# Matmul with rotary embedding on one core: two more block pairs, one queue for all quarter loads, and small warm-up matmuls

## The chip, the cores and the metric

The kernel runs on one core of one Trainium2 chip. The metric is the device time of one execution in microseconds. An execution was also profiled; the profile's span runs from the first to the last instruction, and the rest of the device time lies around it.

The engines go by two names here: PE is TensorE (matmuls; PEld its weight loads), DVE is VectorE, ACT is ScalarE, POOL is GpSimd, SP is SyncE, which issues DMAs and computes nothing.

## The reference

`x` has 16 batches of 512 rows of 768 float32 values, `weight` is 768 x 768, `cos` and `sin` are 512 x 64, and there are 12 heads of 64.

```python
y = np.matmul(x, weight).reshape(batch, seq, n_heads, head_dim)
y1, y2 = y[..., :32], y[..., 32:]
out1 = y1 * cos1 - y2 * sin1
out2 = y2 * cos2 + y1 * sin2
out = np.concatenate([out1, out2], axis=-1).reshape(batch, seq, hidden)
```

`cos1` and `cos2` are the two halves of `cos`, the same for each batch and head; so are `sin1` and `sin2`.

## The kernel before

**Tiles.** The 8192 rows of `x` are 64 tiles of 128 rows, in 16 groups of four (`QB = 4`): tile 4g + s is in group g. A group has the same quarter of the sequence for four batches. A pair is two neighbouring tiles, written (g, h): (6, 0) is tiles 24 and 25, (6, 1) is 26 and 27.

**Two ways to turn a tile.** The contraction needs `x` transposed. An ordinary tile is loaded whole by SyncE into one of `NX` buffers `xs` (`load`), cast to fp16 by ScalarE into `xc` (`cast`), transposed on TensorE with the identity into the PSUM tile `pt`, and copied by ScalarE into `xt` (`turn`, or from tile 6 on `turn_rows`, twelve 64 x 64 transposes on halves of the rows). A *block pair* is loaded in four quarters (`load_quarter`), so placed that a transpose of 32 x 32 blocks on VectorE (`turn_pair`, L303) finishes the work, into one of `NXP` buffers `xp`; it takes no TensorE time and no PSUM. A block pair of SyncE's arrives as float32 in one of `NB` buffers `xb` and is cast by ScalarE into one of two buffers `xd` (`cast_pair`); one of GpSimd's is converted to fp16 by the DMA on its way into one of `NBH` buffers `xh`, and has no cast. `BLOCKS` names the block pairs and who loads them; before, they are (3,1), (5,1), (7,1), (8,0), (8,1), (9,1), (10,0), (10,1), (11,1), (12,1), (13,1) and (15,1) on SyncE, (4,1) and (6,1) on GpSimd.

**Matmuls and products.** From tile 4 on the matmuls (L365, `walk` and `both`) run as two interleaved lines, one on each half of the contraction rows, and fill three PSUM banks per half group, the other three serving the next half; the first and last tiles use L340. When a unit of columns is complete, VectorE multiplies it by cos and sin in one instruction (`rope`, L446), from PSUM into `tq` or the no longer needed `w_raw`. GpSimd adds the two products (L468) into one of four output buffers `ov`; in the last group VectorE and TensorE do some of the sums. ScalarE issues most stores, SyncE the last ones.

**What sets the order.** All is written by hand: `do` appends an instruction to its engine's queue and adds the semaphore waits that its tiles need. The main loop goes over tiles i = 4 to 63 and writes the matmuls of tile i, the block transposes of pairs that begin before tile i + 4 (`B_AHEAD`), turns 3 tiles ahead, casts 5 ahead, and GpSimd's loads 20 ahead. SyncE's loads follow the list `fetch`; `pump` sends on from it as long as a buffer of the kind is written off. Pairs in `EARLY` have their quarters in their tiles' place in that list; other SyncE pairs (`soon`) have theirs spread between the tile loads before.

**The start.** While the first loads are under way, TensorE multiplies zeros (`warm`, L582, the tile `cold`): nine matmuls of 128 x 512, the turn of tile 0, three more, the turn of tile 1. The last six of the twelve also clear the banks that the first matmuls add to. The six weight chunks are cast by VectorE as they land, and the first four tiles' matmuls follow chunk by chunk.

Of the kernel before, what the change touches and what calls it, by code (L numbers as in the profile page):

```python
# [16 lines left out]
class Flow:  # L17
# [24 lines left out]
    def do(self, e, make, reads=(), writes=(), dma=None, tick=True, after=0):  # L42
        need = {}
        for k in reads:
            for s, v in self.wrote.get(k, {}).items():
                need[s] = max(need.get(s, 0), v)
        for k in writes:
            for d in (self.wrote, self.readby):
                for s, v in d.get(k, {}).items():
                    need[s] = max(need.get(s, 0), v)  # L50
        if e == "pe":
            need.pop("pe", None)
            if after:
                need["pe"] = after
        waits = self.settle(e, need)
        for s, v in waits[:-1]:
            self.eng[e].wait_ge(self.sem(s), v)  # L57
        i = make(self.eng[e])
        if waits:
            s, v = waits[-1]  # L60
            i.wait_op(self.sem(s), v, "sem-ge")
        name, step = (dma, 16) if dma else (e, 1)
        self.sem(name)
        self.order[name] = len(self.order) + sum(self.count.values())
        at = self.count[name] + step
        if tick or dma:
            i.then_inc(self.sems[name], step)
            self.count[name] = at
            self.known[name, at] = dict(self.seen[e])
        for k in reads:  # L70
            d = self.readby.setdefault(k, {})
            d[name] = max(d.get(name, 0), at)
        for k in writes:
            self.wrote[k] = {name: at}
            self.readby[k] = {}
        return i
# [32 lines left out]
def kernel(  # L109
# [11 lines left out]
    f = Flow(nc, tc)  # L121
    do = f.do
    P = nc.NUM_PARTITIONS
# [13 lines left out]
    LAST = NG - 1  # L137


    BLOCKS = {}  # L140
    for g in range(5, 14):
        BLOCKS[g, 1] = "pool" if g % 2 == 0 and g >= 4 else "sp"
    BLOCKS[LAST, 1] = "sp"
    BLOCKS[4, 1] = "pool"
    EARLY = ((3, 1), (8, 0), (8, 1), (9, 1), (10, 0), (10, 1), (11, 1), (12, 1), (13, 1))
    for p in EARLY:
        BLOCKS[p] = "sp"

    def sbuf(name, shape, dt):
        return nc.alloc_sbuf_tensor(name, shape, dt).ap()  # L150

    NX, NB, NBH, NC, NCP, NXT, NXP, NOV = 10, 3, 3, 5, 2, 8, 4, 4

    ident = sbuf("ident", [P, P], FP16)
    cold = sbuf("cold", [P, 512], FP16)
# [26 lines left out]
    py = nc.alloc_psum_tensor("py", [P, 6 * 512], FP32).ap()  # L182
# [14 lines left out]
    def where(i):  # L197
        g, s = divmod(i, QB)
        return QB * (g // SB) + s, g % SB

    def pair_of(i):
        return i // QB, (i % QB) // 2

    def is_block(i):
        return pair_of(i) in BLOCKS

# [11 lines left out]
    def load_quarter(gh, q):  # L218
        g, h = gh
        b, r = where(g * QB + 2 * h)  # L220
        e = BLOCKS[gh]
        src = x[b : b + 2].rearrange("b (j a r) (q k) -> r q a (b j) k", r=SB, a=R, q=NQ)
# [282 lines left out]
    def store_half(g, h, c, at):  # L505
# [20 lines left out]
       reads=["ident"], writes=["ident32"])  # L526
# [13 lines left out]
    fetch, quarters = [], []  # L540
    soon = [p for p in sorted(BLOCKS) if BLOCKS[p] == "sp" and p not in EARLY]
    for i in range(QB, NTILE):
# [3 lines left out]
        if not is_block(i):  # L546
            fetch.append(i)
            for _ in range(2 if i == QB * (LAST - 1) else 1):
                if quarters:
                    fetch.append(quarters.pop(0))  # L550
        elif pair_of(i) in EARLY:
            fetch += [(pair_of(i), q) for q in ((0, 2), (1, 3))[i % 2]]
# [23 lines left out]
    WARM = 12  # L576
    warmed = [0]

    def warm(k):
        for _ in range(k):  # L580
            b = warmed[0] % 6
            do("pe", lambda eng: eng.matmul(  # L582
                py[:, ts(b, 512)], cold[:, 0:P], cold, start=True, stop=warmed[0] < WARM - 6),
                reads=["cold"], writes=[f"ps{b}"], tick=False)
            warmed[0] += 1

    def mm0(i, c):
# [10 lines left out]

    U0 = units(0)
    warm(9)  # L600
    castx(0, "act")
    turn(0, "dve")
    castx(1, "act")
    warm(3)
    turn(1, "dve")
    castx(2, "act")
# [13 lines left out]
    for c in CHUNKS[3:5]:  # L620
# [8 lines left out]
        reads=["sin", "csn1", "cos"], writes=["csn"])  # L629
# [74 lines left out]
    for i in range(QB, NTILE):  # L704
        g, s = divmod(i, QB)
# [16 lines left out]
        for n, p in enumerate(pieces(g, s)) if i >= ROWS else ():  # L722
# [3 lines left out]
            for c in CHUNKS:  # L726
                mm_piece(i, p, c, c == CHUNKS[0], c == CHUNKS[-1],
                         tick=c == CHUNKS[-1])
# [60 lines left out]
```

## Time and profile before

| | |
|---|---|
| Time, median of 3 runs | 150.32 us (149.86 to 150.71) |
| The profiled execution's own time | 148.68 us |
| Its span | 146.9 us |
| TensorE, VectorE, GpSimd, ScalarE busy | 140.0, 128.0, 116.7, 76.5 us |
| Granted TensorE clock | 1.00 in all windows |
| Bytes moved | 52.44 MB, mean 357 GB/s |
| DMA issues: whole tiles, quarters, GpSimd's quarters | 36, 48, 8 |

In the page, the groups of instructions give busy time, mean nanoseconds of one, and the idle time of the engine just before them. The chain of waits goes back from the last instruction to what released it. Timelines list start and length of merged runs of instructions; a bracket tells how long the engine had been idle before and what ended that. Windows give each engine's busy time in a stretch, then the granted clock, the share of the DMA engines and GB/s.

### The profile page before, as it was taken

The page shows a single profiled execution, that of the slowest core. Times are in us where ns is not written, and L with a number is a line of the kernel's source. Part 1 is how long each engine was busy: PE and PEld are TensorE (multiplying, and loading weights), DVE is VectorE, ACT ScalarE, POOL GpSimd, SP SyncE. Part 2 cuts the span into 40 slices and gives each one's busy share as a digit, 9 for nine tenths or more (in the row PEclk, how much of TensorE's full clock was granted, in tenths as well). Part 3 has the DMA queues.
Part 4 walks back from the last instruction along what each step waited for, and adds up shares of the span by engine and source line. Part 5 has one row for each costly group of instructions (what it writes and reads, how often), then busy time and mean ns, then how long its engine had stood idle before and what let it go on. Part 6 is the DMA issues. An engine that isn't in the chain of part 4 may idle for free.

```text
span 146.9 us, 4261 instructions
## 1 busy us (share of the span) xinstructions
PE 140.0 (95%) x1846; PEld 112.1 (76%) x1846; DVE 128.0 (87%) x105; ACT 76.5 (52%) x84; POOL 116.7 (79%) x64
## 2 busy tenths in 40 slices
PE   6969999999999999999999999999999999999980
PEld 2445578888888888888888888888888888765860
DVE  0155999878989999899999999999989899999990
ACT  3453798788242933557442942284664649931010
POOL 2000399999996988959788988989899999899980
PEclk9999999999999999999999999999999999999999
DMA  4999999999999999999999999999999999999684
GB/s 118 379 403 404 402 401 270 263 332 327 329 332 330 339 390 389 383 345 375 377 386 384 389 395 387 396 392 393 385 388 398 392 404 401 394 412 360 267 314 158
DMA packets 37826, 52.44 MB, mean 357 GB/s; under 512 B 4656, under 2 KB 31024, under 8 KB 37808
## 3 DMA queue, kind: packets, MB, share of 16 engines
q1 hardware_dynamic: 21200, 30.42, 59.2%
q10 hardware_dynamic: 14432, 20.97, 38.6%
q0 software_dynamic: 2176, 0.79, 4.3%
q8 instruction: 14, 0.23, 0.6%
q14 instruction: 4, 0.03, 0.1%
HBM read 27.79 MB, written 25.17 MB: 361 GB/s over the span
## 4 chain that ended last, share of the span: by engine, by line
PE 83%; DVE 12%; issue 2%; DVEq 0%; SPq 0%
PE py L365 69%; DVE tq L446 8%; PE py L340 5%; PE py L582 4%; PE pt L275 3%; DVE w_raw L446 2%; PE pt L260 2%; DVE ov L415 1%; DVE py L408 0%; DVE xs L408 0%; DVE xt L194 0%; DVE w_sb L194 0%; DVE cold L519 0%; DVEq L57 0%; DVEq L784 0%
## 5 line engine op out<-in xcount | busy, mean ns | idle before, releaser
L468 POOL TENSOR_TENSOR ov<-tq 128x512 f32<-128x512 f32 (+3 forms) x34 | 76.1, 2258 | 22.4 <-DVE tq L446 21.8
L446 DVE TENSOR_TENSOR tq<-py,csn 128x1024 f32<-128x1024 f32 (+2 forms) x51 | 74.2, 1491 | 2.9 <-PE py L365 1.9
L365 PE MATMUL py<-w_sb,xt 64*128 64x512 f16 (+1 forms) x672 | 64.1, 323 | 0.0
L365 PE MATMUL py<-w_sb,xp 64*128 64x256 f16 (+1 forms) x624 | 58.7, 323 | 0.0
L365 PEld LDWEIGHTS py<-w_sb,xt 64*128 64x128 f16 x672 | 47.3, 94 | 8.8 <-DVE tq L446 0.4
L365 PEld LDWEIGHTS py<-w_sb,xp 64*128 64x128 f16 x624 | 44.2, 94 | 7.2
L194 ACT COPY xt<-pt 128x768 f16<-128x768 f16 x34 | 27.1, 801 | 33.2 <-PE pt L275 31.3
L194 ACT CAST xc<-xs 128x768 f16<-128x768 f32 x36 | 32.5, 910 | 18.3 <-PE py L365 10.5
L468 POOL TENSOR_TENSOR ov<-w_raw 128x1536 f32<-128x1536 f32 (+2 forms) x15 | 35.4, 2372 | 3.0 <-DVE w_raw L446 2.9
L446 DVE TENSOR_TENSOR w_raw<-py,csn 128x1024 f32<-128x1024 f32 (+1 forms) x22 | 35.2, 1600 | 2.5 <-PE py L365 2.1
L194 ACT CAST xd<-xb 128x1536 f16<-128x1536 f32 x12 | 19.6, 1632 | 4.0 <-PE py L365 4.0
L340 PE MATMUL py<-w_sb,xt 128*128 128x256 f16 (+1 forms) x102 | 16.8, 317 | 1.1 <-DVE w_sb L194 1.1
L340 PEld LDWEIGHTS py<-w_sb,xt 128*128 128x128 f16 x102 | 9.4, 98 | 6.7 <-DVE w_sb L194 2.0
L275 PEld LDWEIGHTS pt<-ident,xc 64*128 64x128 f16 x360 | 11.6, 95 | 1.2 <-issue 0.2
L275 PE MATMUL pt<-ident,xc 64*128 64x64 f16 x360 | 11.6, 190 | 0.0
L303 DVE STREAM_TRANSPOSE xp<-xd 128x768 f32<-128x768 f32 x12 | 11.6, 966 | 0.0
L582 PE MATMUL py<-cold 128*128 128x512 f16 x12 | 5.5, 630 | 1.4 <-DVE cold L519 1.4
L194 DVE COPY xt<-pt 128x768 f16<-128x768 f16 x2 | 1.1, 558 | 5.8 <-PE pt L260 5.8
L194 DVE CAST w_sb<-w_raw 128x768 f16<-128x768 f32 x6 | 3.3, 557 | 2.7 <-DMA w_raw<-in_weight_dram 2.6
L194 ACT COPY ov<-py 128x256 f32<-128x256 f32 x1 | 0.4, 372 | 10.0 <-PE py L478 10.0
L229 POOL DMA_DIRECT2D xh<-in_x_dram x8 | 4.8, 601 | 0.0
L582 PEld LDWEIGHTS py<-cold 128*128 128x128 f16 x12 | 1.6, 145 | 3.6 <-issue 2.2
(26 smaller groups left out, 24.5 us busy)
## 6 DMA issues: line engine op xcount, KB each, us to landing
out_dram<-ov ACTq DMA_DIRECT2D x53, 384.0 KB, 7.6
xs<-in_x_dram SPq DMA_DIRECT2D x36, 384.0 KB, 11.7
xb<-in_x_dram SPq DMA_DIRECT2D x48, 192.0 KB, 10.5
out_dram<-ov SPq DMA_DIRECT2D x4, 768.0 KB, 6.0
w_raw<-in_weight_dram SPq DMA_DIRECT2D x6, 384.0 KB, 7.0
xh<-in_x_dram POOLq DMA_DIRECT2D x8, 96.0 KB, 15.3
out_dram<-ov SPq DMA_DIRECT2D x1, 384.0 KB, 2.3
out_dram<-ov SPq DMA_DIRECT2D x3, 128.0 KB, 2.1
```

What stands on the lines that cost most here:

```text
L194: eng.copy(out=o, in_=i_) if e == "act" else eng.tensor_copy(out=o, in_=i_)
L229: do(e, lambda eng: eng.dma_start(out=dst[ts(q, R)], in_=src[r, q]), writes=[f"{name}q{q}"], dma=name)
L260: do("pe", lambda eng: eng.transpose(pt[:, t, h, :], src[:, t, h, :], ident), reads=[f"xc{c}", "ident"], writes=[f"pt{k}"], tick=(t, h) == ...
L275: do("pe", lambda eng: eng.transpose(pts[r][:, t, h, :], src[rows, t, h, :], ident[rows, rows]), reads=[f"xc{c}", "ident"], writes=[f"pt{r ...
L303: do("dve", lambda eng: eng.transpose(out=dst, in_=src), reads=rd, writes=[f"xp{z}"])
L340: do("pe", lambda eng: eng.matmul(ps, get(t, h), w_sb[:, t, h, a - s * H : z - s * H], start=start, stop=stop), reads=[key, f"w{t}{h}"], w ...
L365: do("pe", lambda eng: eng.matmul(py[:, a:z], get(t, h)[rows], w_sb[rows, t, h, a - s * H : z - s * H], start=start, stop=not opens and en ...
L415: do("dve", lambda eng: eng.tensor_tensor(out=ov_b[o][:, ds(c0, w)].rearrange("p (h t d) -> p h t d", t=2, d=HD), in0=q.rearrange("p (h t ...
L446: do("dve", lambda eng: eng.tensor_tensor(out=tq.rearrange("p j (h d) -> p j h d", d=D), in0=ps.rearrange("p (h d) -> p h d", d=D) .unsque ...
L468: do(adder, lambda eng: eng.tensor_tensor(out=ov_b[o][:, ds(c0, w)].rearrange("p (h t d) -> p h t d", t=2, d=HD), in0=tq[:, 0].rearrange(" ...
L582: do("pe", lambda eng: eng.matmul(py[:, ts(b, 512)], cold[:, 0:P], cold, start=True, stop=warmed[0] < WARM - 6), reads=["cold"], writes=[f ...
```

## The change

Three parts:

- There are sixteen block pairs instead of fourteen: (6,0) and (12,0) are new, so tiles 24, 25, 48 and 49 are no longer turned on TensorE.
- All are SyncE's. (4,1) and (6,1) move from GpSimd to SyncE and get a cast on ScalarE. All but (15,1) have their quarters in their tiles' place in the list of loads; (5,1) and (7,1) were spread before. The buffers change with it: `xs` 11 instead of 10, `xb` 4 instead of 3, no `xh`. Loads are 32 whole tiles and 64 quarters.
- The first six of the twelve matmuls of zeros become eight each of 64 rows, 64 weight columns and 64 columns.

```diff
-    BLOCKS = {}
-    for g in range(5, 14):
-        BLOCKS[g, 1] = "pool" if g % 2 == 0 and g >= 4 else "sp"
-    BLOCKS[LAST, 1] = "sp"
-    BLOCKS[4, 1] = "pool"
-    EARLY = ((3, 1), (8, 0), (8, 1), (9, 1), (10, 0), (10, 1), (11, 1), (12, 1), (13, 1))
+    BLOCKS = {(LAST, 1): "sp"}
+    EARLY = ((3, 1), (4, 1), (5, 1), (6, 0), (6, 1), (7, 1), (8, 0), (8, 1), (9, 1), (10, 0), (10, 1), (11, 1), (12, 0), (12, 1), (13, 1))
     for p in EARLY:
         BLOCKS[p] = "sp"
...
-    NX, NB, NBH, NC, NCP, NXT, NXP, NOV = 10, 3, 3, 5, 2, 8, 4, 4
+    NX, NB, NBH, NC, NCP, NXT, NXP, NOV = 11, 4, 0, 5, 2, 8, 4, 4
...
     def warm(k):
         for _ in range(k):
             b = warmed[0] % 6
-            do("pe", lambda eng: eng.matmul(
-                py[:, ts(b, 512)], cold[:, 0:P], cold, start=True, stop=warmed[0] < WARM - 6),
-                reads=["cold"], writes=[f"ps{b}"], tick=False)
+            n = 64 if warmed[0] < WARM - 6 else 512
+            for c in range(0, 512, n):
+                do("pe", lambda eng: eng.matmul(
+                    py[0:min(P, n), ds(b * 512 + c, n)], cold[:, 0:min(P, n)], cold[:, ds(c, n)],
+                    start=True, stop=warmed[0] < WARM - 6),
+                    reads=["cold"], writes=[f"ps{b}"], tick=False)
             warmed[0] += 1
```

## The prediction

> **What bounds the kernel now.** I read the page first, then the chain of waits, the timelines of TensorE, VectorE and ScalarE, and a table of windows. The page:
>
> ```profile
> PE 140.0 (95%) x1846; PEld 112.1 (76%) x1846; DVE 128.0 (87%) x105; ACT 76.5 (52%) x84; POOL 116.7 (79%) x64
> PE 83%; DVE 12%; issue 2%; DVEq 0%; SPq 0%
> ```
>
> Busy PE could still hide pauses, so I went to the chain in order of time (start, length, what):
>
> ```profile
> 1.41 4.02 PE py L582 x9
> 5.43 0.64 PE pt L260 x6
> 6.07 1.25 PE py L582 x3
> 7.32 0.35 PE pt L260 x6
> ...
> 66.18 13.65 PE py L365 x126
> 79.83 0.17 PE pt L275 x10
> ...
> 104.11 1.92 PE py L365 x19
> 106.03 0.20 PE pt L275 x11
> 106.23 5.85 PE py L365 x54
> 112.08 0.17 PE pt L275 x10
> ```
>
> From 8.8 to 124.5 us TensorE runs without a break. Where no tile is turned on it, 126 matmuls (seven tiles of 18) take 13.65 us, 1.95 each. Four tiles of which two are turned take 112.26 - 104.11 = 8.15 us instead of 7.80: a turn costs 0.175 us of TensorE. VectorE, the next one, keeps close behind:
>
> ```profile
> 100.51 0.97 DVE L303 STREAM_TRANSPOSE xp<-xd 128x768 f32<-128x768 f32 x1
> 101.40 5.58 DVE L446 TENSOR_TENSOR tq<-py,csn 128x2048 f32<-128x2048 f32 x3
> 107.45 1.23 DVE L446 TENSOR_TENSOR w_raw<-py,csn 128x1024 f32<-128x1024 f32 x1 [0.46 <-PE py L365]
> ...
> 115.60 2.36 DVE L446 TENSOR_TENSOR tq<-py,csn 128x1024 f32<-128x1024 f32 x2 [0.53 <-PE py L365]
> ```
>
> A block transpose holds it 0.89 us (100.51 to 101.40). The brackets are its pauses for TensorE; from 115.60 to the end at 143.3 it has none over 0.15 us. So the end is set by when VectorE reaches that product, and then by TensorE and VectorE in turn.
>
> **The turns that go.** Tiles 24, 25, 48 and 49 become block pairs (6,0) and (12,0). Their 48 small transposes leave TensorE: 4 x 0.175 = 0.70 us, half near 56 to 58 us, half at 104 to 106. All of it lies on the path.
>
> **VectorE.** Two transposes more, 2 x 0.89 = +1.78 us. The two pairs that GpSimd loaded, (4,1) and (6,1), now read xd; theirs fall from 1.17 (60.39 to 61.56) to 0.89, -0.56. (6,0)'s stands behind group 5's first product (55.30): 0.89 goes into the pauses at 59.25 (0.54) and 67.40 (0.27), the 0.28 saved on (6,1) and the overlap; by 100 us VectorE is some 0.3 ahead of before, as TensorE is 0.35. (12,0)'s stands behind group 11's first product: then 107.45 becomes 107.45 - 0.3 + 0.89 - 0.46 - 0.08 = 107.50 (0.08 is what consecutive instructions overlap when nothing waits), with no pause left, and 115.60 becomes 107.50 + 8.15 - 0.53 - 0.08 = 115.04. TensorE's data would be there at 115.60 - 0.70 = 114.90, so VectorE decides: -0.56 us. TensorE waits for VectorE only when a bank is still being read. In group 9, which has two pairs at once behind it, the product of the last two banks ends at 96.01 and the next matmul into them starts at 96.26: 0.25 us to spare. By the same count group 11's, after the change, ends at 111.71 and TensorE wants them at 112.56 - 0.70 = 111.86: 0.15. Bounds of this term: -0.70 (VectorE hidden) to 0 (each transpose given back); I take -0.56, as groups 7 and 9 have the same order of work and show no pause of TensorE.
>
> **ScalarE, GpSimd, SyncE.** ScalarE loses four casts (0.910) and four copies (0.801), -6.84, and gains four pair casts (1.632), +6.53. The new wait: (6,1)'s and (12,1)'s casts need the xd buffer of two pairs before, that is VectorE's transpose; copies, casts and stores on ScalarE queue behind. The like casts at 70.68 and 86.68 waited 2.0 us and TensorE did not pause, so I cost this at nothing; with that cover gone it is at most those 2.0 us once per new pair. GpSimd loses eight DMA issues of 0.60 (24.4 to 32.6 us); its sums there come earlier, but VectorE's pauses follow TensorE, so that is worth nothing. [...]
>
> **The loads.** The windows (last columns: TensorE clock, DMA share, GB/s) and one line of ScalarE:
>
> ```profile
> 20.00:30.00 10.00, 10.00 (x178) 8.58 (x173) 8.80 (x5) 8.66 (x12) 10.00 (x8) 1.00 1.07 302
> 30.00:40.00 10.00, 10.00 (x157) 8.69 (x154) 8.72 (x7) 6.04 (x8) 10.00 (x8) 1.00 1.16 325
> 80.00:90.00 10.00, 10.00 (x137) 8.55 (x133) 10.00 (x9) 6.17 (x5) 9.14 (x3) 1.00 1.07 390
> 117.64 0.91 ACT L194 CAST xc<-xs 128x768 f16<-128x768 f32 x1 [1.47 <-DMA xs<-in_x_dram]
> ```
>
> GpSimd's converting loads run while the rate is 302 to 332; later it is 390, and a group of four tiles (3.15 MB in and out in 8 us) asks for 393. So the transfers never regain the time, and one load is late for ScalarE at 117.64. TensorE doesn't feel it in this execution, so the term is 0 here; the missing 60 to 90 GB/s over 30 us, less 0.8 MB that converted data count half, is about 1.3 MB or 3.4 us of earlier loads. 768-byte pieces instead of whole rows take some back: 381 GB/s at 70 to 80 us against 403 at 10 to 15, 0.2 us for 1.6 MB.
>
> **The start.** Six matmuls of 512 columns start every 0.427 us (nine to 5.23), 2.56 us together; they become 48 of 64 columns. No row shows 64 columns at this slow rate. From below: the turn at 5.43 steps 128 columns in 0.107 us with a new weight load each time, so loads hide and columns count: 48 x 0.0533 = 2.56 us, nothing changes. A gain is excluded but for 0.14 us, since the first tile's cast ends at 5.09 and its turn starts at 5.23, and because later weight chunks set the pace (chunk 3 is cast by 12.27, its first matmul is at 12.38). From above: load and matmul in series, 0.145 (the mean load at L582, 128 columns) + 0.053 = 0.198 each, 9.5 us; the speed-up near 7.2 us, where the turn falls from 0.64 to 0.35, would shorten that, and the start would come some 4 us later. I take the lower end, being nearest to the turn's row (same rows of the array, same kind of load), and 0.05 for the change of shape. A delay x at 5.23 reaches the end as about x/2, because what it pushes beyond 7.2 us runs twice as fast, less 0.2 us of small pauses at 16.4, 18.0 and 18.8.
>
> [...]
>
> **Sum.** -0.56 and 0.0: -0.6 us. The profiled execution's own time is 148.68 (span 146.9, 1.8 around it): 148.1. The median of the three runs is 150.32, 1.6 above, so I put the change on it: 149.7. About 0.5%, 0.75 us, is what a measurement here can tell from no change.
>
> **Rivals.**
> *Small matmuls in series* (slower). A load of half the columns, 0.145/2 = 0.072, not hidden: 0.125 each. By 7.2 us 46 are done, and all that follows runs fast: the second turn starts 1.8 us late, +1.6 at the end after the pauses, net +1.0: 151.3. It decides from 0.087 us per small matmul on (x = 1.6, x/2 - 0.2 = 0.6). For it: a shape no row shows. Against: the turn's row.
> *The fast rate comes later.* It came 5.76 us after the first matmul. If small ones don't count towards it, it comes 2.56 us later, near 9.7: turn 0.3 and half of 8.8 to 9.7 lost, +0.6, net 0: 150.3. Against: three large matmuls and six more follow the small ones anyway. [...]
> *VectorE gives it back.* The 0.15 us margin fails, TensorE waits once per new pair: gain 0 to 0.3, 150.2. Against: groups 8 and 10.
> *Loads were the hidden bound of the longer runs* (faster). If the 1.6 us by which the runs exceed the profiled one are late loads near the end, the 3.4 us won covers them: -1.6, some 148.7. For it: loads land 0.0 to 1.7 us before use from 112 us on. Against: no pause of TensorE here shows it.
>
> **Numbers.** Forecast 0.44, loads 0.23, series 0.20, late rate 0.08, given back 0.05. Faster by over 0.5%: the loads and 0.17 of the forecast's own spread, 0.40. Slower: 0.16 of the series and 0.04 of the late rate, 0.20. The rest 0.40. The range reaches from most of the loads' case to half of the series': 148.5 to 151.0.
>
> **What would show it.** Right: 48 matmuls from 1.41 that end near 4.0, the first turn still at 5.2; seven-tile stretches also around 55 and 105 us; no pause of VectorE near 107; its product of 115.60 at 115.0; GB/s near 390 from 22 us on; no wait of ScalarE for a load after 20 us. Wrong: a first turn after 5.5 us, a bracketed wait of TensorE for VectorE in groups 6 or 12, or an end that moves by over 1 us.

## The result, and the profile after

The changed kernel takes 151.13 us in the median of four runs (151.00 to 152.18), the kernel before 150.09 beside it (148.86 to 150.71). The ratio is 1.0126, interval 1.0078 to 1.0175: slower by 1.3%, where 0.4% faster was forecast. The profiled execution of after has its own time 152.18 and a span of 150.4; it is the slowest of its four, as before's 148.68 lies under the others, so the two traces are 3.5 us apart where the ratio says 1.9, and differences read from them are larger than those of the medians.

The page of after, busy time and the chain by engine:

```profile
PE 139.8 (93%) x1840; PEld 113.6 (76%) x1840; DVE 129.1 (86%) x107; ACT 76.7 (51%) x80; POOL 112.2 (75%) x56
PE 50%; DVE 16%; DMA 14%; SPq 12%; issue 3%; ACT 2%; POOL 0%; ACTq 0%; DVEq 0%; POOLq 0%
```

TensorE is as busy as before in a longer span, and the chain that was PE 83%, DVE 12% now holds DMA and SyncE's queue. Two late transfers stand in it. The first, from the chain in order of time (start, length, what):

```profile
7.32 9.53 DMA xs<-in_x_dram
16.85 0.02 issue
16.88 0.90 ACT xc L190
17.78 0.05 issue
17.82 0.51 PE pt L256 x6
```

Tile 4's load lands at 16.85, is cast 0.02 us later, and its turn begins at 17.82. TensorE's timeline around it, before:

```profile
16.37 0.51 PE L260 MATMUL pt<-ident,xc 128*128 128x128 f16 x6
```

and after:

```profile
1.40 4.14 PE L580 MATMUL py<-cold 128*64 128x64 f16 x51 [1.40 <-DVE cold L515]
5.35 0.52 PE L256 MATMUL pt<-ident,xc 128*128 128x128 f16 x6
...
6.36 0.50 PE L256 MATMUL pt<-ident,xc 128*128 128x128 f16 x6
...
17.82 0.51 PE L256 MATMUL pt<-ident,xc 128*128 128x128 f16 x6 [0.84 <-ACT xc L190]
```

The 48 small matmuls are not slow (they and three large ones end with the first turn at 5.35), and the second turn is even 0.78 us earlier than before's 7.14. What is late is tile 4, the fifth tile. It lands at 16.85, 1.47 us later than before (15.38). Of that 0.91 us lie between it and the load ahead of it, `sin`; `sin` itself lands 0.56 us later (14.96, 14.40 before), which is no mark of the small matmuls: in the fifteen kernels below that don't have 48 of them it lands anywhere from 14.09 to 15.43.

The second late transfer is near the end. ScalarE's timeline, before:

```profile
121.18 0.91 ACT L194 CAST xc<-xs 128x768 f16<-128x768 f32 x1
122.00 1.63 ACT L194 CAST xd<-xb 128x1536 f16<-128x1536 f32 x1
123.53 0.79 ACT L194 COPY xt<-pt 128x768 f16<-128x768 f16 x1
```

and after:

```profile
116.67 1.61 ACT L190 CAST xd<-xb 128x1536 f16<-128x1536 f32 x1 [2.52 <-DMA xb<-in_x_dram]
118.18 0.80 ACT L190 COPY xt<-pt 128x768 f16<-128x768 f16 x1
...
121.59 0.89 ACT L190 CAST xc<-xs 128x768 f16<-128x768 f32 x1 [1.80 <-DMA xs<-in_x_dram]
122.97 0.80 ACT L190 COPY xt<-pt 128x768 f16<-128x768 f16 x1 [0.49 <-PE pt L271]
124.05 0.92 ACT L190 CAST xc<-xs 128x768 f16<-128x768 f32 x1 [0.28 <-DMA xs<-in_x_dram]
125.52 1.60 ACT L190 CAST xd<-xb 128x1536 f16<-128x1536 f32 x1 [0.55 <-DMA xb<-in_x_dram]
127.01 0.81 ACT L190 COPY xt<-pt 128x768 f16<-128x768 f16 x1
```

TensorE's timeline of after has these two bracketed pauses from 100 us on:

```profile
119.13 3.51 PE L361 MATMUL py<-w_sb,xt 64*128 64x512 f16 x40 [1.20 <-ACT xt L190]
127.88 0.35 PE L271 MATMUL pt<-ident,xc 64*128 64x64 f16 x12 [0.88 <-ACT xt L190]
```

The pair cast at 125.52 is that of (15,1). In the trace's landings its last quarter is there at 125.50; before it was there at 121.57, 0.43 us ahead of the cast. The copy of a turned tile stands behind it in ScalarE's queue (127.01), and TensorE waits for that copy at 127.88. The first pause comes the same way: (13,1) lands at 116.65, where it was there at 112.17 before, is cast at 116.67, and TensorE waits at 119.13 for the copy behind that cast (118.18). TensorE is stopped by a load through an engine that is half idle (ScalarE, 51% busy).

The groups of instructions say the same: ScalarE's idle time before pair casts was 4.0 us, ended by TensorE,

```profile
L194 ACT CAST xd<-xb 128x1536 f16<-128x1536 f32 x12 | 19.6, 1632 | 4.0 <-PE py L365 4.0
```

and now loads end most of it:

```profile
L190 ACT CAST xc<-xs 128x768 f16<-128x768 f32 x32 | 28.8, 907 | 20.3 <-DMA xs<-in_x_dram 12.7
L190 ACT CAST xd<-xb 128x1536 f16<-128x1536 f32 x16 | 26.0, 1624 | 16.5 <-DMA xb<-in_x_dram 9.2
```

**A rule that holds in all the traces read.** The last interleaved matmul ends 7.35 to 7.46 us after ScalarE begins the cast of (15,1), and the span ends 17.44 to 17.80 us after that matmul. Where nothing pauses TensorE, that cast begins 103.86 to 103.91 us after the first interleaved matmul (four traces with fourteen pairs); with the 0.70 us of four turns gone it would be 103.17. So each trace can be booked as a start, the turns, and how much later than that the load of (15,1) landed or pauses pushed its cast. From before to after, at the last interleaved matmul (129.40 to 132.92, +3.52): start 18.13 to 19.63, **+1.50**; turns **-0.70**; the cast of (15,1) at 125.52 instead of 19.63 + 103.17 = 122.80, **+2.72**. The brackets show 2.08 of the last; the ends of matmuls are modelled. This booking takes the 0.70 as given; that it is about right is seen from the starts of the interleaved matmuls, each counted from the first of its trace: the one that starts at 113.80 us before is 0.52 us earlier in after, 0.60 in after_bigwarm and 0.67 in before_16pairs (both below). The gain was there, and the late loads took it back.

### The profile page after: what moved, and what is told of

Its sections match the earlier page's. It is cut to its first block, busy times and chain, and to the rows that moved or that the text cites. A ratio compares the mean times of both kernels' runs of the same rounds, so it can differ in the third digit from the quotient of the medians.

```text
span 150.4 us, 4253 instructions
## 1 busy us (share of the span) xinstructions
PE 139.8 (93%) x1840; PEld 113.6 (76%) x1840; DVE 129.1 (86%) x107; ACT 76.7 (51%) x80; POOL 112.2 (75%) x56
## 4 chain that ended last, share of the span: by engine, by line
PE 50%; DVE 16%; DMA 14%; SPq 12%; issue 3%; ACT 2%; POOL 0%; ACTq 0%; DVEq 0%; POOLq 0%
PE py L361 46%; DVE tq L442 9%; DMA xb<-in_x_dram 8%; DMA xs<-in_x_dram 6%; DVE w_raw L442 5%; SPq L210 5%; SPq L225 4%; PE pt L271 2%; SPq L232 2%; ACT xd L190 1%; PE py L336 1%; DVE xp L299 1%; ACT xc L190 1%; PE pt L256 1%; DVE ov L411 1%
## 5 line engine op out<-in xcount | busy, mean ns | idle before, releaser
L361 PE MATMUL py<-w_sb,xp 64*128 64x256 f16 (+1 forms) x720 | 65.4, 323 | 0.0
L361 PEld LDWEIGHTS py<-w_sb,xp 64*128 64x128 f16 x720 | 51.8, 94 | 7.4
L361 PE MATMUL py<-w_sb,xt 64*128 64x512 f16 (+1 forms) x576 | 55.0, 323 | 1.2 <-ACT xt L190 1.2
L361 PEld LDWEIGHTS py<-w_sb,xt 64*128 64x128 f16 x576 | 40.6, 94 | 9.3 <-DVE tq L442 1.9
L190 ACT CAST xc<-xs 128x768 f16<-128x768 f32 x32 | 28.8, 907 | 20.3 <-DMA xs<-in_x_dram 12.7
L190 ACT COPY xt<-pt 128x768 f16<-128x768 f16 x30 | 24.0, 801 | 22.1 <-PE pt L271 20.9
L190 ACT CAST xd<-xb 128x1536 f16<-128x1536 f32 x16 | 26.0, 1624 | 16.5 <-DMA xb<-in_x_dram 9.2
L299 DVE STREAM_TRANSPOSE xp<-xd 128x768 f32<-128x768 f32 x16 | 15.4, 964 | 1.3 <-ACT xd L190 1.3
L580 PE MATMUL py<-cold 128*64 128x64 f16 (+1 forms) x54 | 5.0, 270 | 1.4 <-DVE cold L515 1.4
L580 PEld LDWEIGHTS py<-cold 128*64 128x64 f16 (+1 forms) x54 | 3.2, 151 | 1.9 <-DVE cold L515 1.4
```

The source lines that it names most:

```text
L190: eng.copy(out=o, in_=i_) if e == "act" else eng.tensor_copy(out=o, in_=i_)
L299: do("dve", lambda eng: eng.transpose(out=dst, in_=src), reads=rd, writes=[f"xp{z}"])
L361: do("pe", lambda eng: eng.matmul(py[:, a:z], get(t, h)[rows], w_sb[rows, t, h, a - s * H : z - s * H], start=start, stop=not opens and en ...
L580: do("pe", lambda eng: eng.matmul(py[0:min(P, n), ds(b * 512 + c, n)], cold[:, 0:min(P, n)], cold[:, ds(c, n)], start=True, stop=warmed[0] ...
```

## The experiments

All were timed beside the kernel before on the same chip. The table gives, from each one's profile, the first interleaved matmul, the landing of (15,1), its distance to the first interleaved matmul, and TensorE's pauses after 19 us. One execution is behind each row, the ratios are from all timed runs.

| Kernel | pairs | ratio (interval) | first | (15,1) lands | distance | pauses, us |
|---|---|---|---|---|---|---|
| before | 14 | 1 | 18.13 | 121.57 | 103.44 | none |
| after | 16 | 1.0126 (1.0078 to 1.0175) | 19.63 | 125.50 | 105.87 | 1.20, 0.88 |
| after_bigwarm | 16 | 1.0106 (1.0059 to 1.0152) | 18.54 | 124.72 | 106.18 | 0.77, 1.66 |
| before_smallwarm | 14 | 1.0081 (1.0048 to 1.0115) | 19.98 | 123.69 | 103.71 | none |
| after_14pairs | 14 | 1.0150 (1.0087 to 1.0214) | 19.95 | 123.65 | 103.70 | none |
| before_16pairs | 16 | 1.0060 (1.0027 to 1.0094) | 17.85 | 123.10 | 105.25 | 0.32, 1.26 |
| before_warm128 | 14 | 1.0047 (1.0016 to 1.0078) | 18.35 | 124.11 | 105.76 | 1.52 |
| before_16_latecast | 16 | 1.0094 (1.0061 to 1.0126) | 18.66 | 124.06 | 105.40 | 1.89 |
| before_16_whole | 16 | 1.0007 (0.9978 to 1.0035) | 18.93 | 122.88 | 103.95 | 0.58 |
| before_16_nostore3 | 16 | 0.9995 (0.9966 to 1.0023) | 18.32 | 122.04 | 103.72 | 0.35 |
| after_14_bigwarm | 14 | 1.0033 (0.9998 to 1.0068) | 18.13 | 122.62 | 104.49 | 0.50 |
| after_15_early | 15 | 1.0092 (1.0057 to 1.0127) | 17.82 | 123.02 | 105.20 | 1.52 |
| after_15_late | 15 | 1.0080 (1.0053 to 1.0107) | 18.22 | 124.19 | 105.97 | 0.65, 1.35 |
| before_nostore3 | 14 | 0.9976 (0.9958 to 0.9995) | 19.17 | 120.46 | 101.29 | none |
| before_early57 | 14 | 1.0019 (0.9990 to 1.0049) | 18.61 | 123.30 | 104.69 | 0.71 |
| before_15_pool6 | 15 | 1.0069 (1.0035 to 1.0104) | 18.41 | 123.25 | 104.84 | 0.71, 0.19 |
| before_16_pool | 16 | 1.0227 (1.0178 to 1.0276) | 18.06 | 124.34 | 106.28 | 0.46, 0.50, 1.17 |
| before_pull | 14 | 1.0012 (0.9976 to 1.0048) | 18.30 | 118.64 | 100.34 | 0.43 |

**1. The change with the six large matmuls** (after_bigwarm): the first six matmuls of zeros as before, all else as after.

```diff
-            n = 64 if warmed[0] < WARM - 6 else 512
-            for c in range(0, 512, n):
...
+            do("pe", lambda eng: eng.matmul(
+                py[:, ts(b, 512)], cold[:, 0:P], cold, start=True, stop=warmed[0] < WARM - 6),
```

> The change without its third part: the first six matmuls of zeros are 128 x 512 again. Theory L (late loads alone: the DMA engines are full, and more quarters of 768-byte packets make loads late from 90 us on): the time stays that of the change, 151.1 within 0.4, and ScalarE still waits some 20 us for loads. Theory S (the small matmuls upset the start: loads of the first 10 us came at 334 instead of 383 GB/s and the first interleaved matmul at 19.7 instead of 18.1 us): 149.6 to 150.0, first interleaved matmul back near 18.1.

1.0106, 151.25 us, as theory L had it: most of the loss is there without the small matmuls. The start is earlier by 1.1 us and the distance to (15,1) no shorter.

**2. The kernel before with the small matmuls** (before_smallwarm): the loop of the change in the old kernel.

> The kernel before with the small matmuls alone. Theory L: within 0.4 us of before (150.1). Theory S: 1.0 to 1.5 us slower than before, with the loads of the first 10 us late as in the change.

1.0081, some 1.2 us, with no pause after 19 us: the part alone costs, as theory S had it. In the profile, whose span is 2.2 us longer than before's, a start 1.85 us later makes most of it. Its timeline has the same gap as after's, and larger:

```profile
18.21 0.51 PE L260 MATMUL pt<-ident,xc 128*128 128x128 f16 x6 [1.14 <-ACT xc L194]
```

The two parts each lose, 1.0081 and 1.0106, but together they give 1.0126, not their sum. The traces fit that: after starts 1.09 us later than after_bigwarm and (15,1) lands only 0.78 us later, so TensorE waits less for it.

**3. The change without the two new pairs** (after_14pairs): `(6, 0)` and `(12, 0)` taken out of `EARLY`.

> The change without the pairs (6,0) and (12,0); all fourteen pairs stay SyncE's. A whole tile is 128 packets of about 125 ns, a tile in quarters 512 of about 38: 0.2 us more DMA time per tile on 16 engines. Theory L with the new pairs as its cause: faster than the change by 0.8 or more, ScalarE's waits for loads after 20 us fall below 5 us. Theory Q (the move of (4,1) and (6,1) from GpSimd's queue to SyncE's is the cause): the time of the change within 0.4 us, or slower, since four turns return to TensorE (+0.7).

1.0150, with no pause, start and distance those of before_smallwarm to 0.03 us. The start's loss needs only the small matmuls. But theory L had this kernel 0.8 us or more below the change, 1.0073 or less, and the interval lies above that: no gain from leaving out the new pairs is seen in time, though the intervals are wide. The profiled execution (150.68 us) is one of the shortest of its six (150.49 to 154.93), so that it shows no pause says little of the others; and kernels 5, 10 and 13 pause for late loads without new pairs.

**4. The kernel before with the two new pairs only** (before_16pairs):

```diff
-    EARLY = ((3, 1), (8, 0), (8, 1), (9, 1), (10, 0), (10, 1), (11, 1), (12, 1), (13, 1))
+    EARLY = ((3, 1), (6, 0), (8, 0), (8, 1), (9, 1), (10, 0), (10, 1), (11, 1), (12, 0), (12, 1), (13, 1))
```

> The kernel before with (6,0) and (12,0) as SyncE's pairs in their tiles' place; GpSimd's two pairs, the buffers and the matmuls of zeros as before. Theory L with the new pairs as its cause: slower than before by 0.5 to 1.5 us, with pauses of TensorE behind late loads after 100 us. Theory Q: faster than before by 0.4 to 0.7 us, as the prediction's sum had it.

1.0060, slower as theory L had it. Four turns went, and the last interleaved matmul ends 1.09 us later all the same (130.49 against 129.40) from a start 0.28 earlier. TensorE's pauses:

```profile
116.33 3.51 PE L365 MATMUL py<-w_sb,xt 64*128 64x512 f16 x40 [0.32 <-ACT xt L194]
125.45 0.35 PE L275 MATMUL pt<-ident,xc 64*128 64x64 f16 x12 [1.26 <-ACT xt L194]
```

**5. Twenty-four matmuls of 128 columns** (before_warm128): `n = 128` in the loop of the small ones, in the kernel before.

> The kernel before with the first six matmuls of zeros as 24 of 128 x 128 (36 instructions of TensorE more instead of 84, loads included). In the three kernels with 48 small ones, a 16 KB packet of the instruction queue ran from 14.6 to 15.1 us on (22.1 to 22.9 in the three with large ones), it held one DMA engine for 1.08 us, and the next load, that of tile 4, landed 1.9 to 2.2 us after the one before it instead of 1.0. Theory I (the longer instruction stream moves that packet in front of tile 4's load): the packet now comes near 20 us, where loads land over 1.2 us before use; tile 4 lands 1.0 after sin; the time is within 0.5 us of before. Theory A (the small matmuls themselves slow the loads of the first 8 us, 250 to 285 GB/s at 5 to 7 us): those loads are late as with 48, and the time is 0.5 to 1.2 us over before.

The start is that of large matmuls (tile 4 lands 0.98 us after the load ahead of it, `sin`), as theory I had it, and the loads at 5 to 7 us run at 350 and 341 GB/s, against theory A. The time, 1.0047 or 0.7 us, is more than theory I allowed and within theory A's range. The profile puts it to a late (15,1) that was not expected, in a kernel whose loads are those of before; it is one of the longer executions (150.75 us, median 149.82); see what stays open.

**6. The pair casts one tile later** (before_16_latecast), from kernel 4:

```diff
-            elif i % 2 == 0 and BLOCKS[pair_of(i)] == "sp" and pair_of(i) not in xc:
+            elif i % 2 == 1 and BLOCKS[pair_of(i)] == "sp" and pair_of(i) not in xc:
```

> As before_16pairs, but ScalarE casts a pair one tile later, with its second tile's turn in the order (all pairs but (15,1)). Theory N (a pair needs both of its tiles when its first is due, so its second load is wanted one tile, 2 us, earlier, and ScalarE's copies queue behind the cast that waits): the waits of pair casts after 100 us fall from 1.6 to 3.6 to below 1.6 each, the pause of TensorE at 116 is gone, the one at 125 may stay; 149.2 to 149.9. Theory D (the loads are late because quarters cost more DMA time): the waits move to the next load and the time stays 150.2 to 150.7.

The first pause went, the second grew to 1.89 and the ratio to 1.0094. Where in the queue the cast stands does not cure it: the data are late.

**7. The new pairs loaded as whole rows** (before_16_whole), from kernel 4: two loads of 128 rows of 3072 bytes instead of four quarters of 768-byte pieces.

> As before_16pairs, but the two new pairs are loaded as two whole tiles each, 128 rows of 3072 bytes, into the same buffers; their rows then stand in the wrong places, so tiles 24 to 27 of the new pairs' places hold other sums, and the work on all engines is the same. Theory D (4 x 0.2 us of DMA time for 768-byte packets makes the loads late): the load waits shrink by 0.4 us at (6,0) and 0.8 from (12,0) on, TensorE's two pauses (0.32 and 1.26) fall below 0.8 together, 149.5 to 149.9. Theory N: as before_16pairs, 150.2 to 150.7.

1.0007 against 1.0060, intervals 0.9978 to 1.0035 and 1.0027 to 1.0094. Same bytes, same engine work, other pieces: about 0.5%, that is most of what the two pairs lose, though the intervals overlap a little. The whole rows also need two issues of a pair where the quarters need four; this was not told apart from the size of the pieces.

**8 and 9. Without group 3's stores**, in kernel 4 (before_16_nostore3) and in before (before_nostore3):

```diff
-            store_half(*q, f.count["pe"])
+            if q[0] != 3:
+                store_half(*q, f.count["pe"])
```

> As before_16pairs, but the four stores of group 3's results (1.57 MB, some 3.9 us of the DMA engines near 50 us) are left out. If late loads cause the pauses of TensorE (both theories D and N): the loads from 60 us on land 3 to 4 us earlier, no pause after 100 us, 148.4 to 148.9, below before. If the pauses come from the order of the casts and transposes alone: 150.2 to 150.7 as before_16pairs.

> The kernel before without the stores of group 3 (that group's output is not written). It is the control to the sixteen pairs without these stores. Theory: before has no load that TensorE waits for, so the time on the DMA engines that comes free is worth nothing: ratio 1.000 +- 0.002, no pause, and what the missing stores gave the sixteen pairs was the pauses alone. Rival: fewer stores speed the kernel up in another way, 0.994 to 0.997, and then the sixteen pairs' gain without them says nothing of late loads.

0.9995 from 1.0060, a gain of 0.65%, less than forecast (149.56 us, not 148.4 to 148.9, and a pause of 0.35 stays). The control gains 0.24% itself, a little more than its theory allowed and less than its rival. That leaves some 0.4% for the late loads of the sixteen pairs, and by the intervals it could be nothing. That before gains at all suggests that some of its executions wait for loads as well. In the control's profile no load near the end is late: (15,1) lands 2.57 us ahead of its cast.

**10. The move from GpSimd alone** (after_14_bigwarm): the change without new pairs and without small matmuls.

> The changed kernel with the six large matmuls of zeros and without the two new block pairs: what is left of the change is the move of (4,1) and (6,1) from GpSimd to SyncE, the places of the quarters in the list and the buffers. Theory: the cost of the change is the start (taken out here) and the two new pairs (taken out here). The four moved tiles need less of the DMA engines' time as float32 quarters (1.28 us a tile) than converted on the way (1.57), 1.2 us in all. So no pause of TensorE after 20 us, interleaved matmuls from 18.1 to 18.9, ratio 1.000 +- 0.003. Rival: the move itself takes something, through the order of the list or because quarters and whole rows share SyncE's rings; then TensorE pauses for late loads after 110 us by 0.5 to 1.5 us, ratio 1.004 to 1.010.

1.0033, not told from no change by its interval, and between theory and rival; the one pause of 0.50, at 125 us, is the rival's sign.

**11 and 12. One new pair** (after_15_early has (6,0), after_15_late (12,0)), with large matmuls.

> The changed kernel with the large matmuls of zeros and with only one new pair, (6,0). Theory of transfer time: what counts is how long the transfers before the last loads take in all, wherever the quarters lie; half of the cost and half of the gain of two pairs, so the same ratio as with (12,0) alone, 1.002 to 1.006, with one or two pauses of TensorE after 110 us of 0.5 to 1.3 us in all. Rival, place: the DMA engines catch up between group 6 and the end, and only the late pair costs; then no pause, and the two turns that go give 0.35 us: ratio 0.996 to 0.999.

> The changed kernel with the large matmuls of zeros and with only one new pair, (12,0). Theory of transfer time: as with (6,0) alone, 1.002 to 1.006, pauses of 0.5 to 1.3 us in all after 110 us. Rival, place: the late pair makes all of the cost, so the pauses and the ratio are those of both pairs (2.4 us in the profile, 1.006 to 1.011).

1.0092 and 1.0080: the place makes no difference that the intervals show, so the rival of place falls: the transfers after group 6 give nothing back. Both are above the forecast of half the cost: one pair does nearly as much as two (1.0106), which the theory did not say. The late one's pauses:

```profile
117.33 3.51 PE L361 MATMUL py<-w_sb,xt 64*128 64x512 f16 x40 [0.65 <-ACT xt L190]
126.56 0.35 PE L271 MATMUL pt<-ident,xc 64*128 64x64 f16 x12 [1.35 <-ACT xt L190]
```

**13. The change's order and buffers without the move** (before_early57): (5,1) and (7,1) in their tiles' place, 11 and 4 buffers, (4,1) and (6,1) still GpSimd's.

> The kernel before with the change's places for (5,1) and (7,1) in the list and its 11 and 4 buffers, but (4,1) and (6,1) still loaded by GpSimd. Theory of the third queue: order and buffers cost nothing, so the share of the DMA engines from 20 to 122 us stays near 1.089, the last load lands near 126.0 us, and the ratio is 1.000 +- 0.003. Rival, order: the last load lands near 127.0 and the ratio is 1.003 as for the change with fourteen pairs and large matmuls, with a pause of some 0.5 us near 125.

1.0019, as the theory had it, and so is the share of the DMA engines, 1.088. But (15,1) lands at 123.30 and the last load at 127.68, with a pause of 0.71 at 125.69, as the rival had it. One trace doesn't decide: before_warm128, whose loads are those of before, has its last load at 128.49. The share itself holds over all traces. From 20 to 122 us it is 1.087 to 1.092 in the ten traces of kernels in which GpSimd loads four tiles, 1.100 with six, 1.111 with eight, and 1.068 to 1.072 in the six without (it goes over 1 because packets that overlap in time are each counted). That fits the part of the theory by which some of GpSimd's packet time ran beside the others', so that the move gave it up.

**14 and 15. The new pairs on GpSimd's queue** (before_15_pool6 with (6,0), before_16_pool with both):

```diff
+    BLOCKS[6, 0] = BLOCKS[12, 0] = "pool"
```

> The kernel before with one new pair, (6,0), loaded and converted by GpSimd. Theory of the third queue: four converted tiles take 6.3 us of packet time, of which about 2.1 runs beside the other queues' packets, so some 1.05 us a tile, as much as a whole row tile (1.03). The last load lands near 126.0, two turns go, 0.35 us: ratio 0.996 to 1.000, no pause over 0.3 us. Rival, packet time alone counts: 2 x (1.57 - 1.03) = 1.1 us later loads, ratio 1.003 to 1.006. A second rival: GpSimd's four issues more (2.4 us) delay its sums, and TensorE or VectorE pause for tq before 50 us.

> The kernel before with both new pairs, (6,0) and (12,0), loaded and converted by GpSimd. Theory of the third queue: last load near 126.0, four turns go, 0.7 us, and TensorE then waits for loads for about 0.3 of it: ratio 0.996 to 1.000. Rival, packet time alone: 2.2 us later loads less 0.4 us of slack, ratio 1.007 to 1.012, more than with SyncE's quarters. Second rival: (12,0)'s issues come near 56 us where GpSimd has 90 to 99% busy, its sums then pace VectorE and TensorE pauses for a bank, ratio 1.005 to 1.015.

1.0069 and 1.0227: for two pairs far worse than SyncE's quarters (1.0060). In before_15_pool6 GpSimd's load of (6,1) comes late for VectorE, whose product then holds a bank that TensorE wants. VectorE's timeline of that kernel:

```profile
61.84 1.24 DVE L304 STREAM_TRANSPOSE xp<-xh 128x768 f32<-128x768 f32 x1 [0.60 <-DMA xh<-in_x_dram]
```

and TensorE's:

```profile
65.31 1.68 PE L366 MATMUL py<-w_sb,xp 64*128 64x512 f16 x16 [0.71 <-DVE w_raw L447]
```

This is the "VectorE gives it back" of the prediction, in a kernel it was not made for. In before_16_pool a load of SyncE's is late as well: ScalarE begins a pair's cast at 94.01, when its load lands, VectorE waits 2.24 us for it until 95.64, and TensorE 1.17 us for VectorE until 98.85. For one pair the ratio is a little above what packet time alone was to give (1.003 to 1.006), for two nearly twice it.

**16 and 17. (15,1)'s quarters earlier in the list** (before_pull, after_bigwarm_pull): complete ahead of tile 57's load. In the second the edit against after_bigwarm is only:

```diff
-        if soon and i >= max(2, soon[0][0] - 1) * QB:
+        if soon and i >= max(2, soon[0][0] - 2) * QB:
```

> The kernel before with the same move of (15,1)'s quarters. Theory of the one place: in its profile (15,1) lands 0.43 us before its cast begins; executions in which it lands later gain, the profiled one doesn't, so the ratio is 0.996 to 1.000. Rival: the loads pushed back, (13,1) with 0.86 us to spare and 57 with 0.02, make a new pause near 114 to 119 us, ratio 1.002 to 1.008.

> The change with the large matmuls of zeros, and the quarters of (15,1) up to two places earlier in the list: complete ahead of tile 57's load instead of between 58 and 59. Theory of the one place: (15,1) lands some 2 us earlier, the pause near 127 us (1.66) goes, that near 117.5 stays (0.77) or grows by the half us that (13,1)'s quarters are pushed back: ratio near 1.002, against 1.0106 without the move. Rival, supply: the loads of (13,1), 57 and 58 were used 0.02 us after landing too, so they are late in its place; ratio 1.008 to 1.012, pauses still near 2 us in all.

In before_pull (15,1) lands 4.25 us before its cast, but (13,1), pushed back, now lands at 115.07 and is cast 0.02 us later, and TensorE pauses there:

```profile
117.55 3.51 PE L365 MATMUL py<-w_sb,xt 64*128 64x512 f16 x40 [0.43 <-ACT xt L194]
```

1.0012 in before, which decides for neither theory, and 1.0242 in the change, twice what the rival of supply gave. What makes 1.0242 is not known: the one trace is of an execution of 158.50 us, far from the others (152.4 to 153.9). One place in the list is ruled out for the change; in before, the load that was pushed back is the next to be late.

No version with the whole work in it beats the kernel before.

## Why the prediction was wrong, step by step

**The loads: the step that failed.** "TensorE doesn't feel it in this execution, so the term is 0 here", and the 3.4 us of earlier loads. The term is +2.72 us in the profile of after, and +2.1 in that of before_16pairs by the same booking (its cast at 123.12 against 17.85 + 103.17 = 121.02). Three things in that step were wrong.

The working went by GB/s where a count of transfer time was needed. The column beside it said that the engines were not idle while the rate was low: their share is 1.07 and 1.16 in the prediction's rows from 20 to 40 us. From 20 to 122 us of before, the mean packet of a whole row (3072 bytes) takes 130.6 ns, of a quarter (768 bytes) 39.9, of GpSimd's converting loads 49.0. A tile is 128 of the first, or 512 of either other kind, on 16 engines: 1.04, 1.28 and 1.57 us. The 64 tiles of before then take 36 x 1.04 + 24 x 1.28 + 4 x 1.57 = 74.4 us, and those of after 32 x 1.04 + 32 x 1.28 = 74.2. What GpSimd's four tiles save, four new quarter tiles and four whole tiles less give back: -0.2 us and not -3.4. The prediction had 0.2 us for 1.6 MB of quarters, four tiles; by packets it is 4 x 0.24 = 1.0. 768 bytes in 39.9 ns is 19.2 bytes per ns, 3072 in 130.6 is 23.5.

The windows of after show that the rate did not go to 390 once GpSimd's loads were gone (last column GB/s; 302, 325 and 390 before):

```profile
20.00:30.00 10.00, 10.00 (x169) 8.17 (x168) 7.87 (x6) 9.13 (x13) 7.62 (x4) 1.00 1.07 305
30.00:40.00 10.00, 10.00 (x157) 8.84 (x154) 8.73 (x6) 6.70 (x8) 7.79 (x3) 1.00 1.06 383
80.00:90.00 10.00, 10.00 (x146) 8.82 (x144) 10.00 (x8) 5.55 (x5) 8.60 (x4) 1.00 1.07 370
```

The middle one rose as foreseen, the others did not.

That count takes the 3.4 us away, but it doesn't give the lateness: (15,1) lands 3.93 us later in after, and at before's packet times the loads would be where they were. The traces show what is missing. All packets up to that landing take 129.0 us on 16 engines in before and 131.2 in after. The 2.2 us more are nearly all in the length of whole-row packets, 130.2 ns on average in before and 137.2 in after (4801 of them on 16 engines: 2.1 us; the median from 20 to 122 us is 121 in both, so some are much longer). And the share up to the landing, packet time by 16 engines' time, is 1.061 in before and 1.046 in after, where GpSimd's queue is gone. At before's share, 131.2 us would end at 123.7; so of the 3.93 about 2.1 go with packet time and 1.8 with the share. Why some whole-row packets are longer, and whether that is cause or consequence, no run settles.

Last, the margin was read too kindly. The prediction saw "0.0 to 1.7 us before use" and one cast that waited, but took these for harmless because TensorE had no bracket. The load with a consequence had 0.43 us; taking four turns away uses 0.70 of it before any load is later. So even with loads at their old times the gain would have been 0.43 us or less.

**The rival of the hidden bound** (0.23, 148.7) had the right mechanism and the wrong sign: loads near the end do bound the kernel, and the change made them later.

**ScalarE.** Its sum of work was right (16 pair casts at 1.624). The new wait was priced by the buffer it needs, "at most those 2.0 us once per new pair", behind VectorE. It came from the transfer instead, and what is queued behind it, the copies of turned tiles, was named but "TensorE did not pause" was carried over from casts at 70.68 and 86.68.

**The start: the rate was right, the term not.** 48 small matmuls end as forecast, the first turn is at 5.35 (5.2 forecast), and the rival of matmuls in series is out: TensorE's weight loads from 1.40 run 50 in 2.83 us. The weight loads hide behind these 48 on the same rows: the starts of the matmuls are 0.053 us apart, as are those of the loads. The second rival is out as well: the fast rate came no later. By the length of TensorE's instructions it came at 4.15 to 7.43 us in the traces with large matmuls, at 5.38 to 6.45 in the three with small ones. Among kernels with the same start, those with large matmuls, this point differs by up to 3.3 us; what sets it, no run shows.

The term of 0.0 came out as +1.50 in the profile of after, 0.91 of it between `sin` and tile 4, and as 1.2 us in the times of before_smallwarm. It failed because the prediction asked only what the small matmuls do to TensorE. They are also 84 instructions more (48 and their weight loads for 6 and theirs). The DMA queues from 14 to 16 us, before:

```profile
q1 hardware_dynamic: 297, 0.80, 103.4%
```

and after:

```profile
q1 hardware_dynamic: 290, 0.77, 99.4%
q8 instruction: 1, 0.02, 3.4%
```

One packet of 16 KB of the instruction queue holds one of the 16 DMA engines for 3.4% of 16 x 2 us = 1.09 us. With six large matmuls this packet starts at 21.4 to 23.5 us, with 24 of 128 columns at 18.15, with 48 small ones at 14.61 to 15.05, between the landings of `sin` and tile 4. In the three kernels with small matmuls tile 4 lands 1.89 to 2.19 us after `sin`, in the fifteen others of the table 0.96 to 0.99. The 0.9 to 1.2 us more are about the packet's 1.09. In the trace of after, fifteen of the sixteen landing records of tile 4's load come by 15.92 us, the last at 16.85, and its cast begins at 16.88; of `sin`'s, fifteen come by 14.70 and the last at 14.96, and before, of tile 4's, by 15.32 and at 15.38. One part of the load in sixteen is 0.93 us behind the others, where it was 0.06. That eighteen kernels fall on two sides by this packet's place is a strong sign; a version in which the packet alone moves was not tried.

**The turns and VectorE.** 0.70 on TensorE is right within 0.2: the matmuls near 114 us start 0.52 to 0.67 us earlier in the three traces above. No kernel shows it in its time. Whether VectorE would have decided with -0.56 can't be told, as the late loads came first; in after it has one bracketed pause between 50 and 120 us, 0.41 at 52.59, none near 107, and TensorE has none for a bank.

**GpSimd and SyncE, for which the sum has no term.** Not contradicted in time: 1.0033 (0.9998 to 1.0068) for the move, 1.0019 (0.9990 to 1.0049) for order and buffers.

**What stays open.** Kernels with the same loads differ in the distance to (15,1): 103.44 in before, 103.7 with small matmuls, 104.5 to 105.8 in after_14_bigwarm, before_early57 and before_warm128. By packet time after_14_bigwarm should be 1.1 us earlier than before and is 1.05 later; its packets do take 1.0 us less up to that landing, and its share is 1.044 instead of 1.061. With one profiled execution of each, what part of this is the kernel and what the execution is not settled. Nor is why one new pair costs nearly what two do, nor why the landing of `sin` and the rate from 5 to 7 us differ from trace to trace: 252 to 283 GB/s in the three kernels with small matmuls, 212 to 396 in the fifteen others.

## What to carry to other kernels

Before taking work off the engine that bounds a kernel, ask which load is used just after it lands, who stands behind its user in that engine's queue (here a copy at 127.01 behind the cast at 125.52), and how many tenths of a microsecond are left: that margin caps the gain (here 0.43 us of 0.70). Count transfers by packets times their measured time for each size and queue, not by bytes; a list that trades whole rows for quarter rows pays for each (here 1.28 us a tile against 1.04). And count instructions too: in after, 14 packets of 16 KB ran on the queue that the profile calls "instruction", the first for 1.09 us, and a longer stream seems to have moved that one in front of another load.

## What the runs showed that was not expected

- The instruction queue: packets of 16 KB, the first 1.03 to 1.17 us long. It started at 21.4 to 23.5 us in the traces with large matmuls, at 18.15 with 36 instructions of TensorE more and at 14.61 to 15.05 with 84 more; with 84, the load that lands next came 0.9 to 1.2 us later behind the one ahead of it than in the other kernels.
- GpSimd's converting loads took 49.0 ns a packet in before, where four tiles come that way, against 39.9 for SyncE's quarters; two pairs more on that queue cost 2.3% where SyncE's quarters cost 0.6%.
- The kernel before is bound almost twice: from the first interleaved matmul to the last pair's cast TensorE needs 103.87 us and the loads, in its profile, 103.44. Fewer turns bought with quarters lost (1.0060), bought with whole rows gained nothing (1.0007), and fewer stores alone gave a quarter of a per cent (0.9976).
